# Two transformer blocks with hierarchical experts: the experts worked in pairs, their rows gathered four experts at a time, their weights loaded in 2 MB transfers

## The chip, the core and the metric

One NeuronCore of a Trainium2 chip runs the whole program in one launch. The metric is the device time of that launch in microseconds; lower is better. The kernel before was run three times.

## What is computed

The reference is two transformer blocks, one after the other, on 256 tokens of 1024 features, in float32. The first block has two layers (gated spatial mixing, then forgetting attention, each with attention to a memory and a convolutional feed-forward layer). The second has a gated delta rule and a retention mixer, an output projection, and then the layer that this change is about: a mixture of 64 experts in 8 groups, of which each token uses two.

```python
g_idx = jnp.argmax(hf @ w_router_group, axis=-1)            # one group per token
top_p, top_i = lax.top_k(e_prob, 2)                         # two experts inside it
expert_id = (g_idx[:, None] * 8 + top_i).reshape(-1)
order = jnp.argsort(expert_id); xs = ht[order // 2]
gate = lax.ragged_dot(xs, w_gate, group_sizes)              # [64, 1024, 256]
up   = lax.ragged_dot(xs, w_up, group_sizes)                # [64, 1024, 256]
y    = lax.ragged_dot(jax.nn.silu(gate) * up, w_down, group_sizes)   # [64, 256, 1024]
out  = jnp.zeros_like(ht).at[tok].add(y * weights[order][:, None])
return rms_norm(x + out, final_norm)
```

All 64 experts' weights are read: 3 matrices of 1 MB each, 192 MB in all.

## The kernel before, in words

The program is written tile by tile; a scheduler places the instructions of the dense part, while the experts' loop is issued in the order written (`tc.manual_schedule()`). The dense part (the first block and the second block's mixers) streams 1 MB weight units on the SP queue through a ring of two places (`load_unit`, L104), splits each into a high and a low part on ScalarE and VectorE (L118, L119), and multiplies on TensorE with three products per pair of operands (L246 to L248, L288 to L290, L862 to L864).

The experts (`experts`, from L1390) have places of their own for weights: 22 places of 8 KB per partition (1 MB each). 17 of them lie on the right side of SBUF in six pools (`XGROUPS`), opened in the order `XORDER` as the dense part's tiles there die; two are the dense ring's, two (`XA`) lie where dense tiles end, and the last (`XQ`) lies where the routing's tiles end. `more(n)` issues the loads in the order `seq`: gate and up of expert e, then down of expert e-1. Load i takes place i modulo 22, so it waits on SP until the last reader of load i-22 is done. All these loads are issued at L1446 on the SP queue, one after the other; the last expert's in halves at L1451.

`route` (L1602 on) finds each token's two experts and the token's rank in each, as a key 1024 e + rank (L1716). Then for each expert e, `expert(e)` runs these steps of the class `Experts`, 32 rows (`CAP`) each:

- `pick` (L1768 to L1791, VectorE): a one-hot column for each row, times the norm's factor, and another times the row's weight.
- `rows` (L1793, TensorE L1800): gathers the rows with 8 float32 products, four side by side in the array, each a quarter of the features; ScalarE copies them out (L1803). `rows_T` (L1805): two transposes (L1811) put features on partitions, VectorE applies the gain (L1814).
- `gate_up` (L1818, TensorE L1826): 32 float32 products, [128 x 32] by [128 x 128], four side by side; ScalarE copies them out (L1829).
- `turn` (L1841): a transpose (L1846) and two products that put the rows' weights on every partition (L1848). `act` (L1851): silu on ScalarE (L1856), two multiplications on VectorE (L1857, L1858), which write every row twice.
- `down` (L1862, TensorE L1870): four float32 products, [128 x 64] by [128 x 512], two side by side: 64 columns are 32 rows, each there twice. ScalarE and VectorE (L1874, L1875) make of the two copies a high and a low part.
- `sel` (L1878, GpSimd L1884, L1885): which token each row belongs to. `scatter` (L1888, TensorE L1894): four float32r products add the rows to the sums over the experts, which stay in four PSUM banks.

The order inside `expert(e)` is gate_up(e), rows(e+1), turn(e), act(e), down(e-1), loads, rows_T(e+1), scatter(e-2).

An expert with over 32 rows needs `overflow`, a conditional block between experts 40 and 41 (`EOVF`). It claims five places (`OVT`), so up to there `more` issues five loads fewer than there are places. A float32 product is two instructions in the trace (the 32 products of L1826 are 64), a transpose and a float32r product are one.

`finish` (L1509 on) takes the last norm from the PSUM sums and stores the output.

Of the kernel before, what the change touches and what calls it, by code (L numbers as in the profile page):

```python
# [12 lines left out]
F32 = mybir.dt.float32  # L13
# [23 lines left out]
EARLY = 2  # L37
# [6 lines left out]
XGROUPS = (2, 2, 4, 4, 2, 3)  # L44
XORDER = (2, 3, 1, 4, 0, 5)
XA = 2
XQ = 1
EOVF = 40
OVT = 5
# [4 lines left out]
class Builder:  # L54
# [3 lines left out]
    # ---------------------------------------------------------------- setup  # L58
    def setup(self):
        tc, nc, ctx = self.tc, self.nc, self.ctx  # L60
        self.ring = ctx.enter_context(tc.tile_pool(name="ring", bufs=RING))
# [13 lines left out]
    def dense_pools(self, ctx):  # L75
        tc = self.tc
        self.cp = ctx.enter_context(tc.tile_pool(name="cp", bufs=1))
        self.hps = [ctx.enter_context(tc.tile_pool(name="hpa", bufs=1, side="right"))]
        # the split weights, in two pools: the last units do with the first
# [42 lines left out]
    def mark(self, *engines):  # L122
        """the last instructions so far of engines, for behind()."""
# [4 lines left out]
    def behind(self, marks):  # L128
        """what is traced here is issued behind the marks on their engines."""
# [5 lines left out]
    def rsqrt(self, y, v):  # L135
        """y = v ** -0.5."""
# [20 lines left out]
    def squares(self, src, n, **tag):  # L157
        """the sum of the squares of src(t), [128, n], per token."""
# [13 lines left out]
    def row_bc(self, rs, pool, name):  # L172
        """rs [128 tok, tile] as a row [tok] on every partition."""
# [9 lines left out]
    def rstd(self, src, pool, name):  # L183
        """1 / rms of src(t) [128, 1024]: per token, and as a row on every partition."""
# [3 lines left out]
    def scaled(self, dst, ps, rb, mul=1.0):  # L188
        """dst = ps [128 f, 2, 256 tok] * mul * rb."""
# [11 lines left out]
    def to_feat(self, xn, outs, ks=(0, KC)):  # L201
        """xn(t, k) [128 tok, 128]; outs: (gain [128, 8], (hh, hl))."""
# [9 lines left out]
    def split_feat(self, pt, k0, g, h):  # L212
        """two feature chunks pt [128, 2, 256] under a gain, split."""
# [7 lines left out]
    def x_T(self, gain, h=None, half=None):  # L221
        """the residual under a gain, features on partitions, split; the norm's factor is left to its products."""
# [6 lines left out]
    def x_T_by_half(self, gain):  # L229
        """for the end of an output projection: the next layer's input, half by half."""  # L230
# [9 lines left out]
    def mm_feat(self, ps, w, h, c):  # L240
        """ps [128 f, 256 t] for column chunk c of a unit."""
# [15 lines left out]
    def tok_unit(self, ap, h):  # L257
        """[128 tok, tile, 256 f]; the unit's halves are halves of the contraction."""
# [20 lines left out]
    def out_chunks(self, w, chunks, first, last, halves=(0, 1)):  # L279
        """accumulate feature chunks [(hi, lo)] ([128, 256]) times their rows of a unit, bank by bank."""  # L280
# [11 lines left out]
    def out_last(self, w, chunks, first, nxt):  # L292
        """the last unit: each half of the features joins the residual when it is done."""
# [21 lines left out]
    # ------------------------------------------------------- memory attention  # L315
# [51 lines left out]
    def softmax_parts(self, lg, parts):  # L367
        """lg PSUM [128, n]; parts (start, end) are normalised each; returns SBUF [128, n]."""
# [18 lines left out]
    def attn(self, chunk, q, k, v, parts, done, extra=None, late=False):  # L387
        """two heads of a chunk, in steps: queries and keys of its pair of chunks, v [128, 2, 128]; parts the keys of
# [1637 lines left out]
```

## Time and profile before

| | |
|---|---|
| median of 3 runs | 1313.18 us (1312.6 to 1313.52) |
| profiled execution, span from its first to its last instruction | 1311.2 us |
| median less span (launch and end around the span) | 2.0 us |
| instructions | 29064 |
| TensorE busy | 1218.8 us (93%) |
| TensorE weight loads | 984.9 us (75%) |
| VectorE busy | 824.7 us (63%) |
| ScalarE busy | 579.4 us (44%) |
| GpSimd busy | 201.4 us (15%) |
| read from HBM | 327.21 MB |

Of the profiled execution the page gives the span alone. A busy share is a mean over stages with different limits; the experts are the last 480 us. A PE row of the timeline gives the start of a group of instructions and how long it was in the pipeline; as groups overlap, the difference of two starts is what a group costs.

### The profile page before, as it was taken

The page shows a single profiled execution, that of the slowest core. Times are in us where ns is not written, and L with a number is a line of the kernel's source. Part 1 is how long each engine was busy: PE and PEld are TensorE (multiplying, and loading weights), DVE is VectorE, ACT ScalarE, POOL GpSimd, SP SyncE. Part 2 cuts the span into 40 slices and gives each one's busy share as a digit, 9 for nine tenths or more (in the row PEclk, how much of TensorE's full clock was granted, in tenths as well). Part 3 has the DMA queues.
Part 4 walks back from the last instruction along what each step waited for, and adds up shares of the span by engine and source line. Part 5 has one row for each costly group of instructions (what it writes and reads, how often), then busy time and mean ns, then how long its engine had stood idle before and what let it go on. Part 6 is the DMA issues. An engine that isn't in the chain of part 4 may idle for free.

```text
span 1311.2 us, 29064 instructions
## 1 busy us (share of the span) xinstructions
PE 1218.8 (93%) x12119; PEld 984.9 (75%) x12119; DVE 824.7 (63%) x1845; ACT 579.4 (44%) x1053; POOL 201.4 (15%) x190
## 2 busy tenths in 40 slices
PE   8999999999999999999999999888888888788895
PEld 7889999998888999999889988555454555455553
DVE  6867877777766777777778666544444444334443
ACT  7756555556655655555573444322222222121222
POOL 0100000000200000000322000323333332223230
PEclk9999999999999999999899999999999999899998
DMA  8534455553324655555422377899999999999970
GB/s 289 184 117 170 175 187 190 193 193 131 131 93 139 254 192 189 193 181 195 143 97 97 130 294 297 339 419 418 419 417 419 417 418 418 362 406 418 417 295 33
DMA packets 49753, 330.16 MB, mean 252 GB/s; under 512 B 6704, under 2 KB 8240, under 8 KB 10832
## 3 DMA queue, kind: packets, MB, share of 16 engines
q1 hardware_dynamic: 48512, 326.55, 64.4%
q8 instruction: 97, 1.59, 0.5%
q0 software_dynamic: 528, 1.21, 0.3%
q10 hardware_dynamic: 576, 0.49, 0.1%
q14 instruction: 40, 0.33, 0.1%
HBM read 327.21 MB, written 1.05 MB: 250 GB/s over the span
## 4 chain that ended last, share of the span: by engine, by line
PE 78%; DVE 11%; ACT 5%; DMA 3%; issue 2%; POOL 1%; SPq 0%; DVEq 0%; ACTq 0%; POOLq 0%
PE g L1826 9%; PE bank L1870 9%; PE oacc L288 5%; PE oacc L290 5%; PE oacc L289 5%; PE g L1800 4%; PE g L248 3%; PE g L246 3%; PE g L247 3%; DVE y L1875 3%; PE bank L247 3%; PE bank L246 3%; PE bank L248 3%; ACT hs L1874 3%; PE g L862 2%
## 5 line engine op out<-in xcount | busy, mean ns | idle before, releaser
L119 DVE TENSOR_TENSOR wl<-wraw,wh 128x1024 fp32r<-128x1024 f32 x230 | 282.3, 1230 | 91.3 <-ACT wh L118 90.0
L118 ACT CAST wh<-wraw 128x1024 fp32r<-128x1024 f32 x230 | 240.2, 1051 | 217.1 <-PE g L247 73.6
L1826 PE MATMUL g<-wraw,xw 128*32 128x128 f32 x4096 | 126.8, 276 | 55.2 <-DVE xw L1814 49.8
L1826 PEld LDWEIGHTS g<-wraw,xw 128*32 128x32 f32 x4096 | 109.4, 111 | 82.1 <-DVE xw L1814 74.8
L246 PE MATMUL g<-hh,wh 128*128 128x256 f32 x448 | 126.9, 284 | 0.3 <-ACT hh L216 0.3
L248 PE MATMUL g<-hh,wl 128*128 128x256 f32 x448 | 126.5, 283 | 0.6 <-DVE wl L119 0.6
L247 PE MATMUL g<-hl,wh 128*128 128x256 f32 x448 | 126.3, 282 | 0.0
L1870 PE MATMUL bank<-wraw,hm 128*64 128x512 f32 x512 | 124.0, 605 | 0.9 <-DVE y L1875 0.5
L1875 DVE SCALAR_TENSOR_TENSOR y<-bank,part,hs 128x512 fp32r<-128x512 f32 x64 | 48.1, 751 | 117.0 <-ACT hs L1874 117.0
L1884 POOL TENSOR_SCALAR s<-krow,tgt 128x512 bf16<-128x512 f32 x64 | 106.3, 1660 | 24.1 <-ACT krow L1740 12.0
L1829 ACT COPY gu<-g 128x128 f32<-128x128 f32 x64 | 17.0, 265 | 205.0 <-PE g L1826 205.0
L246 PE MATMUL bank<-hh,wh 128*128 128x256 f32 x352 | 99.2, 282 | 0.0
L247 PE MATMUL bank<-hl,wh 128*128 128x256 f32 x352 | 99.0, 281 | 0.0
L248 PE MATMUL bank<-hh,wl 128*128 128x256 f32 x352 | 99.0, 281 | 0.0
L1857 DVE TENSOR_TENSOR h<-h,bank 128x64 f32<-128x64 f32 x64 | 14.2, 222 | 132.9 <-ACT h L1856 132.9
L1874 ACT ACTIVATE hs<-bank,part 128x512 fp32r<-128x512 f32 x64 | 44.0, 687 | 108.3 <-PE bank L1870 108.3
L1885 POOL TENSOR_TENSOR sl<-s 128x256 fp32r<-128x256 bf16 x64 | 42.7, 667 | 297.9 <-PE mo L1894 297.5
L246 PEld LDWEIGHTS g<-hh,wh 128*128 128x128 f32 x448 | 85.0, 190 | 1.8 <-ACT hh L216 0.5
L248 PEld LDWEIGHTS g<-hh,wl 128*128 128x128 f32 x448 | 85.1, 190 | 0.9 <-DVE wl L119 0.8
L247 PEld LDWEIGHTS g<-hl,wh 128*128 128x128 f32 x448 | 85.0, 190 | 1.1 <-issue 0.2
L862 PE MATMUL g<-hh,wh 128*128 128x256 f32 x272 | 79.8, 294 | 1.9 <-ACT qs L983 1.4
L864 PE MATMUL g<-hh,wl 128*128 128x256 f32 x272 | 77.6, 286 | 1.2 <-DVE wl L119 1.2
(560 smaller groups left out, 2787.4 us busy)
## 6 DMA issues: line engine op xcount, KB each, us to landing
wraw<-in_w_gate_dram SPq DMA_DIRECT2D x63, 1024.0 KB, 16.2
wraw<-in_w_up_dram SPq DMA_DIRECT2D x63, 1024.0 KB, 14.8
wraw<-in_w_down_dram SPq DMA_DIRECT2D x63, 1024.0 KB, 16.9
wraw<-in_a_ffn_in_dram SPq DMA_DIRECT2D x22, 1024.0 KB, 4.8
wraw<-in_b_ffn_in_dram SPq DMA_DIRECT2D x22, 1024.0 KB, 4.8
wraw<-in_w_in_dram SPq DMA_DIRECT2D x16, 1024.0 KB, 5.0
wraw<-in_a_ffn_out_dram SPq DMA_DIRECT2D x11, 1024.0 KB, 4.7
wraw<-in_b_ffn_out_dram SPq DMA_DIRECT2D x11, 1024.0 KB, 4.8
```

Source lines behind the costliest of these rows:

```text
L118: self.nc.scalar.copy(wh, r)
L119: self.nc.vector.tensor_tensor(wl, r, wh.bitcast(F32), op=OP.subtract)
L246: nc.tensor.matmul(ps, wh[:, k], hh[:, k], start=k == 0, stop=False)
L247: nc.tensor.matmul(ps, wh[:, k], hl[:, k], start=False, stop=False)
L248: nc.tensor.matmul(ps, wl[:, k], hh[:, k], start=False, stop=k == KC - 1)
L862: nc.tensor.matmul(ps, wh[:, k], hh[:, k], start=k == 0, stop=False)
L864: nc.tensor.matmul(ps, wl[:, k], hh[:, k], start=False, stop=k == KC - 1)
L1826: nc.tensor.matmul(pg[n * C:(n + 1) * C], xw[:, k % 2, k // 2], ws[n // 2][:, k, n % 2 * P:][:, :P], start=k == 0, stop=k == KC - 1)
L1870: nc.tensor.matmul(py[h * 64:(h + 1) * 64], hm[:, j].rearrange("p a c -> p (a c)"), d3[:, j, h * 512:(h + 1) * 512], start=j == 0, stop=j ...
L1874: nc.scalar.activation(hs, py, AF.Copy, scale=m.part[:, 0:1])
L1875: nc.vector.scalar_tensor_tensor(y, py, m.part[:, 1:2], hs.bitcast(F32), op0=OP.mult, op1=OP.subtract)
L1884: nc.gpsimd.tensor_scalar(s1, m.krow, tgt, None, op0=OP.is_equal)
```

## The change

Weights: gate and up of an expert become one array of 16 KB per partition (`w_gu_2`), and the two down matrices of a pair of experts another (`w_down_2`). One transfer moves 2 MB, in rows of 16 KB. There are 11 places of 16 KB per partition: nine in five pools on the right, one where dense tiles end, one where the routing's tiles end. The ring of the dense part is no longer one of them; it moves into the dense part's pools. The scratch space for descriptors of GpSimd's DMAs shrinks to 1 KB (`SCRATCH`); two of the ten mask planes go, two selector operands being read as broadcast columns of another plane.

```diff
-XGROUPS = (2, 2, 4, 4, 2, 3)
-XORDER = (2, 3, 1, 4, 0, 5)
-XA = 2
-XQ = 1
-EOVF = 40
-OVT = 5
+XGROUPS = (1, 1, 3, 2, 2)
+XORDER = (2, 1, 3, 4, 0)
+XLATE = 1
+PAIRS = 32
+POVF = 20
+OVT = 4
+SCRATCH = 1024
...
-            u64, b64, sel0, sel1 = (cm[:, i] for i in range(4))
+            u64, b64 = cm[:, 0], cm[:, 1]
+            sel0, sel1 = (b64[:, i:i + 1].to_broadcast([P, P]) for i in (0, 64))
...
+            seq = [(0, 0), (1, 0)]
+            for e in range(2, NE, 2):
+                seq += [(e, 0), (e + 1, 0), (e - 2, 1)]
+            seq[-2:] = [(NE - 4, 1), (NE - 1, 0), (NE - 2, 1)]
```

The last two of the 96 loads go in halves of 1 MB. The loop works on pairs:

```diff
+            def pair(p):
+                a, b = 2 * p, 2 * p + 1
+                if p:
+                    X.sel(p - 1)
+                X.gate_up(a)
+                if p < PAIRS - 1:
+                    X.gate_up(b)
+                    if p % 2:
+                        X.gather(p // 2 + 1)
+                    if p > 1:
+                        X.scatter(p - 2)
+                    X.turn(a)
+                    X.turn(b)
+                    X.act(a)
+                    X.act(b)
+                    if p:
+                        X.down(p - 1)
+                else:
...
+                    X.gate_up(b)
+                    X.scatter(p - 1)
+                    X.turn(b)
+                    X.act(b)
+                    X.down(p)
+                more(3 * p + 2 + len(slots) - (OVT if p <= POVF else 0))
...
             with tc.manual_schedule():
-                for e in range(EOVF):
-                    expert(e)
-                    X.pick(e + 2)
-                expert(EOVF)
+                for p in range(POVF + 1):
+                    pair(p)
+                    if p % 2 == 0:
+                        X.pick(p // 2 + 1)
             self.overflow(m, X, [slot() for _ in range(OVT)])
```

The overflow block stands after pair 20 (experts 40 and 41) and claims four places. The steps:

```diff
+    def gather(self, q, n=4):
+        nc, b, s = self.nc, self.b, self.s.pop(q)
+        self.xw[q] = xw = self.kept("xw", NT * n * CAP, [KC, n * CAP], bufs=1)
+        g = b.gain("ffn_norm_2")
+        for i in range(2):
+            ks = range(i * KC // 2, (i + 1) * KC // 2)
+            px = b.bank([P, KC // 2, n * CAP])
+            for k in ks:
+                for t in range(NT):
+                    nc.tensor.matmul(px[:, k - ks[0]], b.x[:, t, k * P:(k + 1) * P], s[:, t], start=t == 0,
+                                     stop=t == NT - 1)
+            nc.vector.tensor_tensor(xw[:, ks[0]:ks[0] + KC // 2], px,
+                                    g[:, ks[0]:ks[0] + KC // 2][:, :, None].to_broadcast([P, KC // 2, n * CAP]),
+                                    op=OP.mult)
...
     def turn(self, e):
-        pt = self.b.bank([P, 5, CAP])
-        nc.tensor.transpose(pt[:, 0:4].rearrange("p a c -> p (a c)"), self.gu, self.b.ident)
-        for t in range(NT):
-            nc.tensor.matmul(pt[:, 4], self.m.onesf, s[:, 3, t], start=t == 0, stop=t == NT - 1)
+        self.pt[e] = pt = self.b.bank([P, 4, CAP])
+        self.nc.tensor.transpose(pt.rearrange("p a c -> p (a c)"), self.gu.pop(e), self.b.ident)
...
+    def down(self, p):
+        hms = [self.hm.pop(2 * p + i) for i in range(2)]
...
+        py = self.b.bank([P, 512], "g")
+        for j in range(2):
+            for n in range(4):
+                h, e = n // 2, n % 2
+                nc.tensor.matmul(py[n * C:(n + 1) * C], hms[e][:, j], d[:, e, j, h * 512:(h + 1) * 512],
+                                 start=j == 0, stop=j == 1)
+        w = self.weight(p)
+        hi, lo = (self.kept(t, o, [512], F32R, 1) for t, o in (("yh", 768), ("yl", 1280)))
+        nc.scalar.activation(hi, py, AF.Copy, scale=w)
+        nc.vector.scalar_tensor_tensor(lo, py, w, hi.bitcast(F32), op0=OP.mult, op1=OP.subtract)
...
+        nc.vector.scalar_tensor_tensor(junk, m.krow, tgt, m.wrow, op0=OP.is_equal, op1=OP.mult,
+                                       accum_out=self.weight(p))
```

So `gather` brings four experts' rows with features on partitions at once (16 float32 products of 128 columns), without copy and transposes; `pick` makes one-hot columns for four experts in six VectorE operations; `sel` also sums each row's weight on VectorE (the diff's last operation); `gate_up` is unchanged but for its operands; `down` does two experts at once, four products of 32 columns side by side; `scatter` adds the high and the low part in eight products per pair. `route` makes a second row array (`wrow`, the weights) beside `krow`, with four more float32 products, and gathers the first four experts before the first pair.

## Rows read from the trace of the kernel before

**Rows 1.** The page's second part: granted TensorE clock, DMA share (tenths) and GB/s in 40 slices of 32.8 us.

```profile
PEclk9999999999999999999899999999999999899998
DMA  8534455553324655555422377899999999999970
GB/s 289 184 117 170 175 187 190 193 193 131 131 93 139 254 192 189 193 181 195 143 97 97 130 294 297 339 419 418 419 417 419 417 418 418 362 406 418 417 295 33
```

**Rows 2.** Busy time by stretch: start and end in us, length, busy us of each engine with its instructions, then granted clock, DMA share, GB/s. The first is the end of the mixers, in which the experts' places open; the next four are the experts; then two earlier stretches.

```profile
747.00:834.00 87.00, 81.91 (x624) 71.39 (x622) 58.80 (x199) 38.77 (x65) 4.40 (x11) 1.00 0.76 292
840.00:1120.00 280.00, 246.21 (x3857) 144.91 (x3855) 121.76 (x389) 60.11 (x155) 87.02 (x75) 1.00 1.01 417
1120.00:1160.00 40.00, 31.10 (x422) 18.08 (x426) 14.31 (x46) 7.10 (x18) 11.77 (x11) 0.91 0.92 362
1160.00:1260.00 100.00, 88.46 (x1382) 51.91 (x1374) 43.05 (x138) 21.67 (x56) 31.73 (x28) 1.00 1.01 418
1260.00:1270.00 10.00, 8.43 (x171) 5.73 (x175) 5.34 (x18) 1.56 (x5) 4.64 (x4) 1.00 0.90 362
640.00:660.00 20.00, 16.28 (x112) 15.21 (x111) 13.82 (x47) 10.80 (x18) 5.68 (x2) 0.83 0.31 110
10.00:20.00 10.00, 9.53 (x67) 9.16 (x67) 9.64 (x34) 9.53 (x17) 0.65 (x1) 1.00 0.93 336
```

**Rows 3.** Timeline of TensorE over one expert in the loop: start, time in the pipeline, instructions; in brackets the idle time before and what ended it.

```profile
1029.92 1.95 PE L1826 MATMUL g<-wraw,xw 128*32 128x128 f32 x64 [0.87 <-DVE xw L1814]
1031.69 1.04 PE L1800 MATMUL g<-x,s 128*32 128x256 f32 x16
1032.67 0.33 PE L1846 MATMUL bank<-ident,gu 128*128 128x128 f32 x1
1032.83 0.53 PE L1848 MATMUL bank<-s,onesf 128*128 128x32 f32 x4
1033.29 1.94 PE L1870 MATMUL bank<-wraw,hm 128*64 128x512 f32 x8
1035.16 0.44 PE L1811 MATMUL bank<-ident,xr 128*128 128x128 f32 x2
1035.53 0.73 PE L1894 MATMUL mo<-y,sl 64*128 64x512 f32 x4
1037.14 0.43 PE L1826 MATMUL g<-wraw,xw 128*32 128x128 f32 x8 [0.88 <-DVE xw L1814]
```

**Rows 4.** The largest sum of waits of TensorE between 840 and 1270 us: who for whom, us in total, times, longest.

```profile
PE g L1826 <- DVE xw L1814: 49.8, 57, 0.9
```

**Rows 5.** The SP queue's issues of the experts' loads: the gate matrices by line (count, ns of one, first and last start); then from the timeline, with the start of each, ten issues in a row (the first and the last) and those on both sides of the overflow block.

```profile
L1446 SPq DMA_DIRECT2D wraw<-in_w_gate_dram x63: 327/328/426, 423.9 to 1235.9; - x63
...
1073.31 0.33 SPq L1446 DMA_DIRECT2D wraw<-in_w_gate_dram  x1
...
1095.76 0.33 SPq L1446 DMA_DIRECT2D wraw<-in_w_gate_dram  x1
...
1114.74 0.33 SPq L1446 DMA_DIRECT2D wraw<-in_w_up_dram  x1
1131.88 0.33 SPq L1446 DMA_DIRECT2D wraw<-in_w_down_dram  x1
```

**Rows 6.** TensorE at the same place, the last step before the block and the first after it, and the chain that ended last there (start, us, what).

```profile
1122.13 0.73 PE L1894 MATMUL mo<-y,sl 64*128 64x512 f32 x4
1128.21 3.64 PE L1826 MATMUL g<-wraw,xw 128*32 128x128 f32 x64 [5.35 <-DMA wraw<-in_w_up_dram]
1131.60 0.69 PE L1800 MATMUL g<-x,s 128*32 128x256 f32 x4
...
1114.74 13.46 DMA wraw<-in_w_up_dram
```

**Rows 7.** TensorE at the end of the routing and the start of expert 0, and the SP queue's last load before.

```profile
827.27 1.07 PE L1800 MATMUL g<-x,s 128*32 128x256 f32 x16 [0.37 <-DVE late L1727]
829.10 1.06 PE L1738 MATMUL bank<-ident,key 128*128 128x128 f32 x8
830.08 1.96 PE L1826 MATMUL g<-wraw,xw 128*32 128x128 f32 x64
...
826.37 0.33 SPq L1446 DMA_DIRECT2D wraw<-in_w_up_dram  x1
```

**Rows 8.** The end: the last expert's last matrix and its scatter, which the last norm follows up to the span's end.

```profile
1296.02 1.94 PE L1870 MATMUL bank<-wraw,hm 128*64 128x512 f32 x8 [0.28 <-issue]
1299.61 0.73 PE L1894 MATMUL mo<-y,sl 64*128 64x512 f32 x4 [1.65 <-DVE y L1875]
```

**Rows 9.** The page's third part (queue, kind: packets, MB, share of 16 engines) and three lines of its sixth (issues: count, KB each, median us from issue to landing).

```profile
q1 hardware_dynamic: 48512, 326.55, 64.4%
q8 instruction: 97, 1.59, 0.5%
wraw<-in_w_gate_dram SPq DMA_DIRECT2D x63, 1024.0 KB, 16.2
out_dram<-x SPq DMA_DIRECT2D x3, 256.0 KB, 3.0
g<-in_final_norm_dram POOLq DMA_DIRECT2D x4, 128.0 KB, 4.3
```

**Rows 10.** The longest wait of TensorE between 640 and 660 us.

```profile
PE sm L1123 <- DVE rsc L1105: 3.2, 1, 3.2
```

More of the change, by code (lines that the diff above doesn't have):

```diff
@@ L36 @@
 NLATE = 6
-EARLY = 2
 T2 = 3
@@ L1431, in experts @@
+            early = len(slots)
             taken = itertools.count()
-            def place(pool, tag):
-                return pool.tile([P, 2048], F32, name="wraw", tag=tag)
             def slot():
-                return place(*slots[next(taken) % len(slots)])
+                return slots[next(taken) % len(slots)].tile([P, 4096], F32, name="wraw", tag="wraw")
             def more(n):
-                while len(m.loads) < min(n, 3 * NE):
+                while len(m.loads) < min(n, len(seq)):
@@ L1455, in experts @@
-            xa = ctx.enter_context(tc.tile_pool(name="moea", bufs=XA, reuse_waits="tile"))
-            slots[-1:-1] = [(xa, "wraw")] * XA
-            more(len(slots))
+                    t = m.loads[e, k] = slot()
+                    if i < len(seq) - 2:
+                        src = A["w_down_2"][e // 2] if k else A["w_gu_2"][e]
+                        with self.behind(self.mark(nc.sync) if 0 < i < early else []):
+                            nc.sync.dma_start(t, src)
+                        continue
@@ L1504, in experts @@
-                X.scatter(NE - 1, True)
+                for p in range(POVF + 1, PAIRS):
+                    pair(p)
+                    if p % 2 == 0 and p < PAIRS - 2:
+                        X.pick(p // 2 + 1)
+                X.scatter(PAIRS - 1, True)
                 self.finish(m, X, m.fin)
@@ L1722, in route @@
         sums(SV[2])
-        X.pick_rows(0)
-        X.rows(0)
+        X.pick(0)
+        X.gather(0)
         sums(SV[3])
@@ L1862, in down @@
-    def down(self, e):
-        nc, m = self.nc, self.m
-        hm = self.hm.pop(e)
-        d3 = self.load(e, 2).rearrange("p (k f) -> p k f", k=2)
-        py = self.b.bank([P, 512])
-        for j in range(2):
-            for h in range(2):
-                nc.tensor.matmul(py[h * 64:(h + 1) * 64], hm[:, j].rearrange("p a c -> p (a c)"),
-                                 d3[:, j, h * 512:(h + 1) * 512], start=j == 0, stop=j == 1)
-        hs = self.wk.tile([P, 512], F32R, name="hs", tag="hs", bufs=1)
-        y = self.kept("y", 640, [512], F32R)
-        nc.scalar.activation(hs, py, AF.Copy, scale=m.part[:, 0:1])
-        nc.vector.scalar_tensor_tensor(y, py, m.part[:, 1:2], hs.bitcast(F32), op0=OP.mult, op1=OP.subtract)
-        self.yy[e] = y
@@ L1888, in scatter @@
-    def scatter(self, e, last=False):
+        junk = self.wk.tile([P, 2, S], BF, name="junk", tag="junk", bufs=1)
+        nc.vector.scalar_tensor_tensor(junk, m.krow, tgt, m.wrow, op0=OP.is_equal, op1=OP.mult,
+                                       accum_out=self.weight(p))
+    def scatter(self, p, last=False):
         nc = self.nc
-        sl, y = self.sl.pop(e), self.yy.pop(e)
+        sl, y = self.sl.pop(p), self.yy.pop(p)
         for t in range(NT):
-            for h in range(2):
-                hs = slice(h * 64, h * 64 + 64)
-                nc.tensor.matmul(self.m.oacc[t][h], sl[hs, t * P:(t + 1) * P], y[hs], start=False, stop=last)
+            for i in range(2):
+                for h in range(2):
+                    hs = slice(h * 64, h * 64 + 64)
+                    nc.tensor.matmul(self.m.oacc[t][h], sl[hs, t * P:(t + 1) * P], y[i][hs], start=False,
+                                     stop=last and i == 1)
```

262 lines of the change are left out of this document (102 added, 160 removed).

## The prediction

> **What bounds the kernel now.** I read the slices first, then the stretches, then one expert in the timeline, then the SP queue, then the end. The slices show two regimes: up to about 750 us the DMA engines are half idle, from about 850 they move 417 to 419 GB/s in nearly every slice, the one dip being at 1115 to 1180 [rows 1]. So the experts' stage (830 to 1300 us, over a third of the time) seems bound by its loads. The timeline says otherwise. One expert takes TensorE 1037.14 - 1029.92 = 7.22 us and it never waits for a load, only 0.87 us per expert for VectorE's gain, 49.8 us in all [rows 3, 4]. The loads are a little slower: ten issues in a row that waited only for earlier loads stand (1095.76 - 1073.31) / 9 = 2.494 us apart, so three matrices take 7.48 us [rows 5]. TensorE gains 0.26 us per expert on a stock of loaded places, and the stock lasts but for one stop, at the overflow block: the last load issued before it (1114.74) lands at 1128.21, and that is when TensorE goes on, after 5.35 us idle; no load is issued from 1114.74 to 1131.88 [rows 5, 6]. After it loads stay ahead. They end near 1269 (the stretch 1260 to 1270 still moves 362 GB/s [rows 2]), while TensorE works until 1299.61 + 0.73 = 1300.3 and the span ends at 1311.2 [rows 8]. **Two limits of nearly equal length lie side by side; today TensorE ends last, 42 us behind the loads.** A change to TensorE's work can win no more than that lag, less what must follow the last byte.
>
> **TensorE's work, per pair of experts.** A group's cost is the difference of starts [rows 3], unless said otherwise.
> - Gate and up: as before, 2 x 1.77 = 3.54.
> - Gather: 16 products, 32 instructions, for four experts. The nearest row is the float32 products of the key, 8 instructions in 0.98 us [rows 7], so 3.92, per pair 1.96. What goes are L1800 (0.98 per expert, the same array work), the two transposes (0.37) and the wait for the gain (0.87).
> - Turn: the transposes stay, 2 x 0.16; the weights' products (0.46 per expert) go.
> - Down: 16 instructions instead of 8 per expert. Two side by side cost 1.87 for 8. The gate products already run four side by side at 1.77/64 us per 128 columns, which is 1.77 for these 16; without any gain from four it would be 3.74. I take 1.87.
> - Scatter: eight per pair, today four per expert, so unchanged: 2 x 0.73 = 1.46 at most.
>
> Sum 9.15 us per pair, today 14.43. Upper bound with a down that gains nothing and two waits like today's: 12.8. The other engines have room whatever the new steps cost: today VectorE is busy 121.76 of 280 us, GpSimd 87.02, ScalarE 60.11 [rows 2], and all three lose steps per expert (GpSimd does its two once per pair); VectorE gains one, the weights' sum.
>
> **The loads become the bound.** 192 units of 1024 KB (1.049 MB, below "units") remain, now moved two at a time. I follow them to their end.
> - Start. The places hold 22 units before and after. The first loads go out at 424 us [rows 5], the others as the mixers end (DMA share 0.76 from 747 to 834 [rows 2]), and before the last place's load is issued at 826.37 [rows 7]. I take the same openings; all 22 units are then in by the time an expert ends, so an earlier place brings nothing. The first place comes free later: the first gather starts at 827.3 as now, takes 3.9 us for four experts, the key's and the weights' 16 instructions take 2.0, gate and up of expert 0 start at 833.2 instead of 830.08, and its place is free at 835.0 [rows 7].
> - From there 170 units are left: 170 x 2.494 = 424.0 us. The fixed part of a transfer counts once: 256 KB land in 3.0 us [rows 9], of which 0.6 is bytes, so 2.4.
> - Rows of 16 KB instead of 8: no row shows a weight load with them. A stretch with rows of 4 KB and less among the others moved 336 GB/s at share 0.93, 361 at a full share, against 417/1.01 = 413 [rows 2]: shorter rows cost 13%, small ones included. A gain of up to 3% (13 us) is the one end. The other is the instruction loads on queue 8, 97 packets of 16.4 KB at 0.005 x 16 x 1311.2 / 97 = 1.08 us [rows 9], 15 GB/s per engine where queue 1 has 24; these run beside queue 1's packets, which they must wait for, so the end is excluded as a likely price and kept as a rival. I take 0, nearest to the spacing row.
> - Overflow. Today the stop costs the DMA engines (418 - 362) x 40 / 418 = 5.4 us [rows 2]. After the change more(n) allows seven loads (14 units, 14 x 2.494 = 35 us) beyond pair 20, so TensorE will stand about that long until all have landed, as it did for one unit today. It has the slack, but nothing is under way when it starts again: load 69 needs the place of expert 42, free 3.7 us after the restart as today (1131.88 - 1128.21). Places come back at TensorE's pace, two units at a time; I add 2 us: 7.4. Ends: 0 and 20 (a whole pair at the low clock plus a landing).
>
> Last landing: 835.0 + 2.4 + 424.0 + 7.4 = 1268.8, about where the loads end today.
>
> **After the last byte.** Today 15.2 us pass from the last down's first product to the end [rows 8]. Now the last half of a down, four abreast, is 0.93 instead of 1.87; eight scatters instead of four add about 0.4. TensorE will have waited before it. Here the trace shows what waits do: after a wait of 3.2 us between 640 and 660 the mean clock of that stretch is 0.83 [rows 2, 10], after the 5.35 us the 64 gate products take 3.39 us instead of 1.77 [rows 3, 6], the low level (1.2 of 2.4 GHz). I add 1.9 for the end at the low level: 16.5. **Span 1268.8 + 16.5 = 1285.3, that is 25.9 less than the profiled 1311.2.** The median of the runs stands 2.0 us above that span, so 1287.
>
> At nothing I cost: the two broadcast columns (four small products), the mask planes, the ring's new address; the two units that the dense ring holds cover them. GpSimd's smaller descriptor space could hold up its seven loads; the nearest row is 4.3 us to landing for a norm's gain [rows 9]: 0 to +5, taken 0, as TensorE has the mixers' products beside it.
>
> The Trainium skill (DMA: Bandwidth & Descriptors, Bandwidth) gives 425 GB/s for a 16 MB transfer and 341 for one of 1 MB, issued from GpSimd; by its 425 the 170 units (178.3 MB) would take an estimated 419.5 us, 4.5 less than taken, and the end would be 1283. The trace has 418 with 1 MB transfers already, as they queue behind each other [rows 2].
>
> **Rivals.**
> 1. *The places starve the loads* (18%). A place of two units opens only when all that lay there is dead, and after the overflow TensorE hands back places too slowly. For it: the share of 0.76 before 834 shows that openings limit the start [rows 2]. Against: 22 units by 835 need only 55 us of DMA time. Price: 20 instead of 7.4 at the block, or up to 7 us at the start; about 1300.
> 2. *TensorE at the low clock* (6%), the one on the other side. Now every load is waited for, 5 us apart, with gaps near 3 us. If the array stays at 1.2 GHz, a pair costs 9.15 x 3.39/1.77 = 17.5 us and TensorE is the bound: 833.2 + 32 x 17.5 + 11.6 (scatter to end [rows 8]) = 1404.8, 1407 with the 2.0. It decides from a mean of (1311.2 - 833.2 - 11.6) / 32 = 14.6 us per pair on, about 65% of the time at the low level. Against: a TensorE that falls behind has no gaps, and in the busy stretches after both stops the clock is back at 1.00 [rows 2]. The Trainium skill (TensorE: Matmul & The Clock Gate, HAM oscillation) describes this case: groups of matmuls shorter than the wait for the next load each start throttled. By that rule alone all pairs would cost the low price; the two stops agree with it, the stock of places speaks against its lasting.
> 3. *The long rows are slower* (4%). Then the transfer doesn't do what it is named for. At queue 8's price it would be far slower, 178.3 MB at 16 x 15.2 GB/s being 733 us; it takes a rate 6% lower (424 us become 450) to eat all that is won. I give half of this to no change.
>
> **How the numbers follow.** My forecast has 72%: 1287, by itself 1275 to 1297. Its low side: no loss at the block (-7.4), no low clock at the end (-1.9), a little from the longer rows. Rival 1 carries the range upward to 1304, a full gain from the rows (13 us) downward to 1273; outside lie rivals 2 and 3 and the tails. This kernel's runs can tell 0.2% (2.6 us) from no change. Faster: 72 + 18 + 2 of rival 3 = 92%; same 2%; slower 6%.
>
> **What would show it.** Right: the stretches from 840 on at 418 GB/s or more but for one dip near the overflow block; TensorE busy well under the 88% of today; its waits now for loads, not for VectorE; in one pair groups of about 3.5, 1.9, 1.5 us; gather beginning near 827; the last load landing 16 to 17 us before the end; some slices with a clock below 1. Wrong: a load rate that differs by over 3%; waits of SP for places in mid-stage; TensorE without waits, or slices at the low clock one after the other; an end over 20 us after the last landing; a dense part that no longer ends near 820.

## The result, and the profile after

| | before | after |
|---|---|---|
| median of the runs | 1312.89 us (4 runs) | 1282.74 us (4 runs, 1282.48 to 1283.66) |
| ratio | | 0.9778, 95% interval 0.9758 to 0.9798 |
| span of the profiled execution | 1311.2 us | 1280.9 us |
| first gather, seen in the trace | 827.27 us | 828.23 us |
| from the first gather to the span's end | 483.9 us | 452.7 us |

The change is 30 us faster; forecast were 26, and 1287 us. The last row matters below: the dense part ahead of the experts ends at another time in each profiled execution (the first gather starts anywhere from 823.2 to 830.5 us in the runs of this study), so kernels that differ only in the experts' stage are compared from the first gather on.

The page's second part, 40 slices of 32.0 us (answers to [rows 1]), and the fourth part, the chain of work that ended last:

```profile
PE   7999999999999999999989999989876767577665
...
PEclk8999999999999999999989999999997998888987
DMA  8524555554323665555523146889999999999994
GB/s 279 201 99 167 190 178 192 194 176 158 132 100 132 239 258 196 176 188 187 186 93 132 67 170 239 334 356 423 425 425 425 426 425 426 422 424 426 426 424 186
...
DMA 11%; PE 2%; DVE 0%; ACT 0%; issue 0%; DVEq 0%; ACTq 0%; SPq 0%
```

TensorE's busy digits fall to 5 to 7 from some 930 us on; from 840 to 1120 us it is busy 74% of the time (first row below), where [rows 2] have 88%. The chain that ended last is DMA with 11% of the span and TensorE with 2%. It goes back no further than the overflow block (the last 13% of the span), while in the kernel before it covers the whole span, TensorE having 78% and DMA 3%. The dip of 362 GB/s is gone. Stretches (columns as in [rows 2]):

```profile
840.00:1120.00 280.00, 208.37 (x3582) 156.28 (x3578) 69.19 (x204) 32.17 (x104) 46.61 (x42) 0.91 1.01 425
1120.00:1160.00 40.00, 29.25 (x494) 20.93 (x486) 9.08 (x27) 5.37 (x16) 6.96 (x7) 0.87 1.01 425
1160.00:1250.00 90.00, 62.28 (x1020) 46.69 (x1020) 19.56 (x57) 9.35 (x30) 13.39 (x12) 0.89 1.01 425
1250.00:1260.00 10.00, 8.29 (x100) 5.91 (x101) 1.60 (x5) 1.76 (x4) 0.67 (x1) 0.83 0.85 347
1260.00:1270.00 10.00, 8.17 (x104) 4.20 (x102) 1.46 (x5) 2.27 (x6) 0.00 (x0) 1.00 0.24 95
```

425 GB/s from 840 to 1250 without a break, where [rows 2] have 417 and 362. TensorE's longest sums of waits from 840 to 1270 (who for whom, us, times, longest), where [rows 4] had VectorE's gain:

```profile
PE g L1817 <- DMA wraw<-in_w_gu_dram: 81.7, 34, 3.3
PE g L1855 <- DMA wraw<-in_w_down_dram: 11.1, 10, 1.7
PE g L1817 <- DVEq L1543: 9.7, 1, 9.7
PE g L1817 <- issue: 5.8, 5, 1.8
```

93 us of waits for loads: TensorE has slack. (DVEq L1543 is VectorE's sequencer at the branch of the overflow block; "issue" is idle time for which the profile shows no reason.) One pair in TensorE's timeline (as [rows 3]; L1817 gate and up, L1801 gather, L1885 scatter, L1835 turn, L1855 down):

```profile
986.66 3.64 PE L1817 MATMUL g<-wraw,xw 128*32 128x128 f32 x64 [3.35 <-DMA wraw<-in_w_gu_dram]
990.23 4.32 PE L1801 MATMUL bank<-s,x 128*128 128x128 f32 x32
994.47 0.50 PE L1885 MATMUL mo<-yh,sl 64*128 64x512 f32 x2
...
995.60 0.44 PE L1835 MATMUL bank<-ident,gu 128*128 128x128 f32 x2
995.96 1.92 PE L1855 MATMUL g<-wraw,hm 128*32 128x512 f32 x16
997.71 1.93 PE L1817 MATMUL g<-wraw,xw 128*32 128x128 f32 x64
1001.20 1.95 PE L1817 MATMUL g<-wraw,xw 128*32 128x128 f32 x64 [1.57 <-DMA wraw<-in_w_gu_dram]
```

Down for two experts costs 997.71 - 995.96 = 1.75: four abreast gain what they gain in the gate. Behind the wait of 3.35 us the gate takes 3.57 us instead of 1.8, the low level; before the pair is over the clock is back. The end (as [rows 8]): the last half of the last down, then the last scatter.

```profile
1266.01 1.07 PE L1855 MATMUL g<-wraw,hm 128*32 128x512 f32 x8 [0.36 <-DMA wraw<-in_w_down_dram]
...
1269.29 0.40 PE L1885 MATMUL mo<-yl,sl 64*128 64x512 f32 x2
```

The last load has landed when TensorE goes on at 1266.0, and 14.9 us later the span ends. **The loads now set the end.**

### The profile page after: what moved, and what is told of

It is laid out like the page before. It is cut to its first block, busy times and chain, and to the rows that moved or that the text cites. A ratio compares the mean times of both kernels' runs of the same rounds, so it can differ in the third digit from the quotient of the medians.

```text
span 1280.9 us, 26452 instructions
## 1 busy us (share of the span) xinstructions
PE 1134.8 (89%) x11231; PEld 985.9 (77%) x11231; DVE 727.4 (57%) x1501; ACT 531.7 (42%) x958; POOL 122.0 (10%) x126
## 5 line engine op out<-in xcount | busy, mean ns | idle before, releaser
L1817 PE MATMUL g<-wraw,xw 128*32 128x128 f32 x4096 | 152.3, 310 | 97.4 <-DMA wraw<-in_w_gu_dram 81.7
L1817 PEld LDWEIGHTS g<-wraw,xw 128*32 128x32 f32 x4096 | 135.8, 125 | 128.7 <-issue 117.9
L248 PE MATMUL g<-hl,wh 128*128 128x256 f32 x448 | 126.3, 282 | 0.0
L1803 DVE TENSOR_TENSOR xw<-bank,gains 128x512 f32<-128x512 f32 x32 | 22.1, 692 | 133.4 <-PE bank L1801 133.4
L864 PE MATMUL g<-hl,wh 128*128 128x256 f32 x272 | 77.6, 286 | 0.0
L1843 DVE TENSOR_TENSOR hm<-h,bank 128x64 f32<-128x64 f32 x64 | 11.6, 218 | 115.2 <-ACT h L1842 115.2
L597 DVE SCALAR_TENSOR_TENSOR hc<-hr,cw,hc 128x254 f32<-128x254 f32 (+1 forms) x176 | 73.5, 478 | 0.8 <-ACT hc L594 0.7
L1855 PE MATMUL g<-wraw,hm 128*32 128x512 f32 x512 | 62.6, 598 | 11.1 <-DMA wraw<-in_w_down_dram 11.1
L1860 DVE SCALAR_TENSOR_TENSOR yl<-g,wr_m,yh 128x512 fp32r<-128x512 f32 x32 | 24.0, 751 | 81.6 <-ACT yh L1859 81.6
## 6 DMA issues: line engine op xcount, KB each, us to landing
wraw<-in_w_gu_dram SPq DMA_DIRECT2D x63, 2048.0 KB, 39.2
wraw<-in_w_down_dram SPq DMA_DIRECT2D x31, 2048.0 KB, 39.2
```

Source lines behind the costliest of these rows:

```text
L248: nc.tensor.matmul(ps, wh[:, k], hl[:, k], start=False, stop=False)
L597: nc.vector.scalar_tensor_tensor(hv[:, c, sh:], hr[:, c, :S - sh], cw[:, 2 - sh, f:f + 1], hv[:, c, sh:], op0=OP.mult, op1=OP.add)
L864: nc.tensor.matmul(ps, wh[:, k], hl[:, k], start=False, stop=False)
L1817: nc.tensor.matmul(pg[n * C:(n + 1) * C], xw[:, k], ws[:, n // 2, k, n % 2 * P:][:, :P], start=k == 0, stop=k == KC - 1)
L1855: nc.tensor.matmul(py[n * C:(n + 1) * C], hms[e][:, j], d[:, e, j, h * 512:(h + 1) * 512], start=j == 0, stop=j == 1)
L1860: nc.vector.scalar_tensor_tensor(lo, py, w, hi.bitcast(F32), op0=OP.mult, op1=OP.subtract)
```

## The experiments

**1. TensorE alone.** In both kernels the later loads are left out, and with them the right weights: experts multiply with what lies in a few places.

```diff
# kernel after
+                    if i >= early:
+                        m.loads[e, k] = m.loads[seq[4 + i % 6]]
+                        continue
# kernel before
+                    if i >= n0:                          # n0 = 21
+                        m.loads[e, k] = m.loads[seq[5 + i % 16]]
+                        if e == NE - 1 and not k:
+                            m.fin = slot()[:, :D]
+                        continue
```

> The kernel after with only the first ten 2 MB loads; every later expert multiplies with weights that already lie in one of six of those places. What is left is TensorE's own pace. My theory (the pair costs TensorE about 9.15 us, and the loads set the end of the kernel after): 32 pairs from 833 us on at 9.15 us, 12 us behind them and some 6 us at the overflow block, a span of 1140 to 1150 us against 1280.9. Rival A (TensorE falls to the low clock and stays there, 17.5 us per pair): 1405. Rival B (TensorE still sets the end, the gain came from elsewhere): no shorter than 1275.

> The kernel before with only the first 21 loads; every later expert multiplies with weights that already lie in one of 16 of those places. My theory (TensorE ends last in the kernel before, its loads run ahead): 7.22 us per expert as before, a time of 1306 to 1313, that is at most 0.6% under the kernel before. If the loads set the end of the kernel before: about 42 us less or more than that is not possible from the lag, but every wait for a load would go; a loads-bound kernel would fall by far over 2%. A second question hangs on it: with no load in flight at the overflow block, a stop of TensorE that stays near 5.4 us belongs to the branch itself, one that goes belonged to a load's landing (the prediction took it so).

Measured: 1135.85 us (one run, span 1134.2) for after, 1310.65 for before (ratio 0.9991, 0.9978 to 1.0005). Without its loads the kernel before takes its usual time: it was bound by TensorE. The kernel after falls by 147 us: it is bound by loads. Its span lies 6 us under the expected range, as TensorE's pairs are shorter than taken. TensorE's timeline of after without loads, two gathers two pairs apart being the period's ends:

```profile
1040.04 3.84 PE L1804 MATMUL bank<-s,x 128*128 128x128 f32 x32
...
1057.70 2.50 PE L1804 MATMUL bank<-s,x 128*128 128x128 f32 x20
```

17.66 / 2 = 8.83 us per pair; predicted were 9.15.

**2. More work on TensorE, first dose.** Each product of gate and up twice; then those of down twice as well.

```diff
# a_gate2, in gate_up
+        for _ in range(2):
             for k in range(KC):
                 for n in range(4):
...
# a_gate2_down2, in down as well
-        for j in range(2):
+        for j in (0, 1, 0, 1):
             for n in range(4):
```

> The kernel after with every product of gate and up done twice (3.54 us more of TensorE per pair, 113 us in all; same result). My theory (loads at 4.92 us per 2 MB, 14.76 per pair, set the pace; TensorE with 9.15 + 3.54 = 12.7 per pair stays under it): only the first expert's doubled products show, the first place coming free 1.8 us later, and perhaps as much after the last byte: 1284 to 1288. Rival (TensorE's work or its waits set the pace): 1282.7 + 113 = 1396, or a good part of it.

> The kernel after with the products of gate and up and those of down done twice (3.54 + 1.75 us more per pair: 14.4 us, the 14.43 of the kernel before). My theory: TensorE then ends last again. From 833 us 32 pairs at 14.4, some 6 us at the block, 12 to 15 us behind them: a span of 1312 to 1316, so the time of the kernel before comes back (1313 to 1318) although the loads move as in the kernel after. Rival (the gain came from the 2 MB loads): at most 1290.

Measured: 1354.39 (ratio 1.0306) and 1377.85 (1.0516). Both expectations missed, by 66 and 60 us beyond their upper ends. TensorE's products have no wait for a load left, but pauses with no releaser, here at 999.67, 1009.29 and 1015.42 (doubled gate and up; the sum is from 840 to 1330):

```profile
999.67 1.07 PE L1818 MATMUL g<-wraw,xw 128*32 128x128 f32 x13 [2.60 <-issue]
...
1004.90 2.58 PE L1818 MATMUL g<-wraw,xw 128*32 128x128 f32 x87
1009.29 3.70 PE L1818 MATMUL g<-wraw,xw 128*32 128x128 f32 x128 [1.81 <-issue]
1015.42 1.45 PE L1818 MATMUL g<-wraw,xw 128*32 128x128 f32 x41 [2.43 <-issue]
```

```profile
PE g L1818 <- issue: 69.1, 38, 3.2
```

In the records of the single packets a 16 KB packet of the instruction queue (queue 8) starts at 997.21, 1006.89 and 1013.16, and TensorE goes on 2.3 to 2.5 us behind each. The same holds of all 25 pauses of its products over 1.5 us from 840 to 1330 (the block's stop aside): each ends 2.2 to 2.6 us behind the start of such a packet. So a new theory: TensorE had run out of instructions, which come over the DMA engines that the weights keep full.

**3. The same dose in few instructions, and the first dose without loads.** Down done three times, then four times; and the doubled gate and up of experiment 2 with the edit of experiment 1.

```diff
# a_down3 (a_down4: * 4), in down
-        for j in range(2):
+        for j in (0, 1) * 3:
             for n in range(4):
```

> The kernel after with the products of down done three times: 3.5 us more of TensorE per pair, the same dose as the doubled gate and up, but in 32 instructions of 512 columns per pair in place of 128 of 128 columns. Theory 1 (the loads set the pace, and the doubled gate and up fell short of it because TensorE waited for its own instructions, which come in packets of 16 KB over the DMA engines that the loads keep full): TensorE's own time would be 1135.9 + 32 x 3.5 = 1248, under 1282.7, so the time stays at 1282 to 1288 and TensorE's idle time without a releaser stays near the 6 us of the kernel after. Theory 2 (any 3.5 us more of TensorE per pair costs, as TensorE's waits add to its work): about 1354, as with the doubled gate and up.

> Down done four times: 5.25 us more per pair, 14.1 us in all, about the 14.43 of the kernel before. Theory 1: TensorE's own time is 1135.9 + 32 x 5.25 = 1304, now over 1282.7, so TensorE ends last: 1304 to 1312, most of what the change had won is gone with the loads as they are. Theory 2: 1385 or more. If the gain came from the 2 MB loads: at most 1290.

> Gate and up done twice, and the loads after the first ten left out (later experts use weights that already lie in six of the places). Theory 1 (TensorE's pauses without a releaser in the doubled gate and up are its instruction loads queueing with the weight loads): they vanish with the weight loads, 1135.9 + 113 = 1249. Theory 3 (the pauses belong to the long run of 256 products itself, whatever the DMA engines do): they stay, some 70 us more, about 1320.

Measured: 1287.40 (0.9822, 0.9799 to 0.9845), 1309.84 (0.9988, 0.9971 to 1.0005) and 1252.93 (one run). All three as theory 1 has it. TensorE's longest wait between 840 and 1270 with down three times, the first stretch with down four times (columns as in [rows 2]), and TensorE in the doubled gate and up without loads, where the 256 product instructions of a pair run without a break:

```profile
PE g L1817 <- DMA wraw<-in_w_gu_dram: 17.2, 8, 3.3
```

```profile
840.00:1120.00 280.00, 278.01 (x4336) 161.65 (x4324) 63.83 (x189) 30.68 (x100) 44.20 (x40) 1.00 1.01 425
```

```profile
980.61 7.17 PE L1821 MATMUL g<-wraw,xw 128*32 128x128 f32 x256
```

So 3.5 us more per pair, 112 us in all, cost 5 us, and from the first gather on 7.8 (1285.1 - 824.61 = 460.5): the last load is issued 408.3 us behind the first gather, 407.8 in the kernel after, and what is added lies behind it, where the last two downs are done three times (7 us). TensorE's waits shrink instead. At 5.25 us more, 14.1 per pair, TensorE ends last again and the time of the kernel before is back, though the loads move 425 GB/s from 840 to 1120. The gain is TensorE's, up to the point where the loads take over. The first dose cost more than its work because of its instructions: the pauses go when the weight loads go. From the first gather on the doubled gate and up takes 524.7 us beside the loads and 421.6 without. Of these 103 us the pauses are 69; an estimated 20 more are products at the low clock behind them (the mean granted clock is 0.95 from 840 to 1330, against 0.99 from 840 to 1240 without loads). The rest is open.

**4. The overflow block left out** (its places are still claimed; no expert here has over 32 rows).

```diff
-            self.overflow(m, X, [slot() for _ in range(OVT)])
+            [slot() for _ in range(OVT)]
```

> The kernel after without the conditional overflow block (its four places are still claimed, so that the loads' places are the same; the experts with more than 32 rows would lose them, but none has). My theory now: the stop of TensorE at the block costs nothing in the kernel after, as eight loads are under way and the loads go on: 1281.5 to 1283. The prediction's step (the block costs the loads 7.4 us): 1275.

Measured: 1281.48 (0.9765, 0.9749 to 0.9782); from the first gather to the end 1282.5 - 829.70 = 452.8, after 452.7. The block costs nothing. Why, in the trace of after (SP's issues around the block, TensorE and VectorE there; columns as before):

```profile
1086.00 0.33 SPq L1442 DMA_DIRECT2D wraw<-in_w_down_dram  x1
1090.90 17.12 SPq L1442 DMA_DIRECT2D wraw<-in_w_gu_dram  x2
```

```profile
1096.10 1.92 PE L1855 MATMUL g<-wraw,hm 128*32 128x512 f32 x16 [1.67 <-DMA wraw<-in_w_down_dram]
1107.74 5.13 PE L1817 MATMUL g<-wraw,xw 128*32 128x128 f32 x128 [9.72 <-DVEq L1543]
```

```profile
1107.57 0.75 DVE L1875 SCALAR_TENSOR_TENSOR junk<-krow,tgt,wrow 128x512 bf16<-128x512 f32 x1 [6.23 <-DVEq L1543]
```

TensorE stands 9.7 us, not 35, and not for a load: behind the stop it runs two experts' gates without a break, though their loads land some 4.9 us apart. By the trace it waits for VectorE, which idles 6.2 us at the branch of L1543; TensorE, VectorE and SP all go on within 0.2 us of each other, so which of them held the others is inferred, not shown. Without loads TensorE still stands 6.2 us there (first line below). SP issues nothing for 16.8 us (its second issue is at 1107.70), but a load takes 39.2 us from issue to landing, eight under way, and the DMA engines do not notice: their share from 1090 to 1108 is 1.01. The branch in three other traces (TensorE behind it in after without loads; then VectorE behind it: before, before without loads, after without loads):

```profile
PE g L1820 <- DVEq L1546: 6.2, 1, 6.2
```

```profile
1128.97 0.17 DVE L1779 TENSOR_SCALAR kk<-key 128x4 f32<-128x4 f32 x1 [5.29 <-DVEq L1540]
```

```profile
1123.73 0.17 DVE L1785 TENSOR_SCALAR kk<-key 128x4 f32<-128x4 f32 x1 [2.54 <-DVEq L1546]
```

```profile
1017.23 0.29 DVE L1792 TENSOR_SCALAR s<-s,rs_m 128x128 f32<-128x128 f32 x1 [3.28 <-DVEq L1546]
```

5.3 and 6.2 us beside the weight loads, 2.5 and 3.3 without. The other traces agree: 6.1 to 6.3 us where loads fill the DMA engines at the block (down three times, rows of 8 KB, shorter look-ahead), 3.2 to 3.9 where few or none are under way there (down four times and the three runs with the doubled gate). TensorE stops at the block in the kernel before without loads, too: the two experts on both sides take 20.07 us (from 1114.03 to 1134.10) instead of 2 x 7.22, in the kernel before 21.49 (1116.52 to 1138.01). So 5.6 of the 7.0 us that it loses there are the branch's, without any load; that the load of [rows 6] landed as it went on is at most a small part of it.

**5. Rows of 8 KB in the kernel after.**

```diff
-                            nc.sync.dma_start(t, src)
+                            for c in (slice(0, 2048), slice(2048, 4096)):
+                                nc.sync.dma_start(t[:, c], src[:, c])
```

> The kernel after with each 2 MB place filled by two transfers in rows of 8 KB instead of one in rows of 16 KB; all else as in the kernel after. Theory 1 (a row of 16 KB takes 612 to 614 ns on a DMA engine, two of 8 KB 2 x 312, and that is all there is to the longer rows): 2.494 instead of 2.460 us per MB, 170 of them, 5.8 us more: 1287 to 1290, 418 GB/s in the experts' stretches. Rival (the gain of the change came from the 2 MB transfers): most of the 30 us gone, 1305 or more. If the rows do nothing at all: 1282 to 1283.

Measured: 1285.44 (0.9806, 0.9785 to 0.9826); from the first gather on 1288.0 - 829.00 = 459.0, 6.3 more than after. The median is a little under the expected range, and its interval overlaps that of the change, so the reading rests on the profiled executions; those of after, of experiment 4 and of experiment 6 agree within 0.1 us. The stretch that answers to the first of the fence on stretches:

```profile
840.00:1120.00 280.00, 215.58 (x3536) 155.38 (x3536) 67.38 (x201) 32.31 (x105) 45.26 (x41) 0.90 1.01 418
```

418 GB/s again. The long rows are worth 1.7% of rate and 6 us, a fifth of the gain.

**6. A shorter look-ahead.**

```diff
-                more(3 * p + 2 + len(slots) - (OVT if p <= POVF else 0))
+                more(3 * p + 2 + len(slots) - 6)
```

> The kernel after with loads issued at most as far ahead as six places less than there are, from the first pair to the last (in the kernel after: four less up to the overflow block, none behind it), so that two to five loads are under way at the end instead of eight. Theory U1 (the DMA engines have rates of their own, packets of 612 to 621 ns, and the slowest sets the last landing however deep the queue is): the same time within 2 us, the issues a little further apart (4.95 to 4.97 us) and the engines done closer together at the end. Theory U2 (the deep queue lets the engines drift apart and costs the last landing some 5 us): 1277 to 1279. Rival 1 of the prediction (too few places starve the loads): 1290 or more, with dips of the DMA share in mid-stage.

Measured: 1279.33 (0.9763, 0.9742 to 0.9783), but in the profiled execution 1277.0 - 824.20 = 452.8 from the first gather on, as after: its gain lies ahead of the experts. And the edit did not do what I meant: TensorE goes on with the last load, issued at 1232.07, at 1262.20, 30.1 us later, 29.9 in the kernel after. `more` only fixes the order of SP's issues; when they go out, the places decide. It says nothing on U1 and U2.

**7. The start.** First the rearrangement with a gather of 64 columns, then a smaller one.

```diff
# a_start
-        X.gather(0)
+        X.gather(0, cols=slice(0, 2 * CAP))
...
                     X.gate_up(b)
+                    if not p:
+                        self.rows_of_keys(m)
+                        X.gather(0, cols=slice(2 * CAP, 4 * CAP))
# a_early
                 X.gate_up(a)
+                if not p:
+                    self.rows_of_keys(m)
```

`rows_of_keys` holds the loop that made `krow` and `wrow` at the end of `route`.

> The kernel after with its start rearranged: the first gather brings only the first pair's 64 columns, expert 0 and 1 follow at once, and the key's and the weights' rows and the other 64 columns come behind them. Theory (the stream of loads stands still from 832 us until the first place comes free at 837.3, and everything behind it hangs on that): the first place is free at 833 to 834, the last landing and the end come 3 to 4 us earlier, 1278 to 1280. Rival (the loads' end is set by the DMA engines' total work and the gap at the start is filled by loads that are still landing): 1282 to 1283.

> The kernel after with one step moved: the products that make the key's and the weights' rows (16 instructions, 2.0 us) stand behind the first expert's gate and up, not among them; the first gather stays whole, with 128 columns. Theory (the stream of loads stands still until the first place is free, and this rearrangement of the start, unlike the one with 64 columns, leaves TensorE no narrow products and no new wait ahead of it, so its granted clock stays at 1.00): the first place comes free 2.0 to 2.4 us earlier (6.7 to 7.1 us behind the start of the first gather, not 9.1), and the span's end stands 450.3 to 450.7 us behind the start of the first gather, not 452.7; the time falls by 2 us, about 1280.5, which the medians alone can hardly show. If the start does not matter: 452.7 us again. If the clock falls as it did with 64 columns: 453 to 455.

Measured: 1281.46 (0.9772, 0.9751 to 0.9794) and 1279.72 (0.9756, 0.9735 to 0.9777); from the first gather on 454.6 and 451.2. TensorE there, of after, of the first and of the second:

```profile
828.23 2.02 PE L1801 MATMUL bank<-s,x 128*128 128x128 f32 x16 [0.77 <-DVE s L1789]
...
833.02 1.06 PE L1817 MATMUL g<-wraw,xw 128*32 128x128 f32 x26
834.01 1.16 PE L1746 MATMUL bank<-ident,key 128*128 128x128 f32 x8
835.00 1.06 PE L1746 MATMUL bank<-ident,w 128*128 128x128 f32 x8
835.99 3.04 PE L1817 MATMUL g<-wraw,xw 128*32 128x128 f32 x102
```

```profile
828.25 1.97 PE L1812 MATMUL bank<-s,x 128*128 128x64 f32 x16 [0.77 <-DVE s L1794]
830.74 3.50 PE L1812 MATMUL bank<-s,x 128*128 128x64 f32 x16 [0.52 <-DVE xw L1814]
834.16 5.44 PE L1828 MATMUL g<-wraw,xw 128*32 128x128 f32 x128
```

```profile
825.86 2.02 PE L1805 MATMUL bank<-s,x 128*128 128x128 f32 x16 [0.77 <-DVE s L1793]
...
830.65 1.95 PE L1821 MATMUL g<-wraw,xw 128*32 128x128 f32 x64
832.53 1.16 PE L1518 MATMUL bank<-ident,key 128*128 128x128 f32 x8
```

The first bought nothing: 64 columns took as long as 128 for the first eight products (1.97 against 2.02), then the granted clock stood at 0.62 from 830 to 834 and 0.53 to 838, and the first place came free at 837.87. The second kept the clock at 1.00: the first place is free 832.66 - 825.86 = 6.8 us behind the first gather, 9.1 in the kernel after, and of these 2.3 us 1.4 reach the end (expected 2.0 to 2.4; the last scatter ran at the low level). Its ratio is the lowest here (that of experiment 6 is 0.9763, at a median of 1279.33), but its interval overlaps that of the change, and the 1.4 us rest on one profiled execution of each.

## Why the prediction was right, and where not

- **What bounds before.** Right, and shown: without loads nothing changes (experiment 1).
- **TensorE per pair.** 9.15 taken, 8.83 measured. Down at 1.75 (1.87), scatter 995.60 - 994.47 = 1.13 (1.46 at most), turn 0.36 (0.32), gate and up as before.
- **The loads become the bound.** Right, shown by experiments 1 and 3. The working from 827.3 gave the last landing 441.5 us behind the first gather; it came 437.7 behind it. The pieces of that, one by one:
  - Start. First place free 7.7 us behind the first gather, measured 9.1: the gather takes 4.8 (833.02 - 828.23) instead of 3.9, 0.78 of it a wait for the gain between its halves, and the first gate with the two rows' products 4.3 instead of 3.8 (up to the issue at 837.33). +1.4. That all was in by then was right: the DMA share from 834 to 838 is 0.02. The issue for the first free place:

```profile
837.33 2.08 SPq L1442 DMA_DIRECT2D wraw<-in_w_gu_dram  x2
```

  - **Rows of 16 KB, taken at 0.** Twelve loads on, SP's issues stand (1205.36 - 1146.30) / 12 = 4.92 us apart (rows below), 2.461 us per unit against 2.494: 170 x 0.033 = -5.6, inside the end of -13 that the text kept.

```profile
1146.30 0.33 SPq L1442 DMA_DIRECT2D wraw<-in_w_down_dram  x1
...
1205.36 0.33 SPq L1442 DMA_DIRECT2D wraw<-in_w_down_dram  x1
```

  - **Overflow block, taken at 7.4: the step that failed.** It said that TensorE stands some 35 us until all issued loads have landed and that nothing is under way then. The runs show a stop of 9.7 us that comes with the branch, loads that never stop, and the same time without the block, 452.8 us against 452.7 (experiment 4). The error was to take the releaser that the chain of waits infers in [rows 6] for the cause, and to read the DMA engines' dip of the kernel before, where 13 us of loads were under way, into one with 39. -7.4.
  - The end of the stream, not in the sum. The DMA engines do not finish together: their mean share falls to 0.85 in the last stretch but one and to 0.24 in the last (fence above). 9.1 + 85 x 4.92 + 2.4 = 429.7 against 437.7, so about +8.0. That the engines' own rates do it (single packets take 612 to 621 ns) is argued, not shown; rows of 8 KB, with 20 us between the last issue and its use instead of 30, have such an end too (a share of 0.59 from 1265 to 1270). The last two loads, in halves, go in rows of 4 KB: their packets take some 161 ns, four of them 644 where one of 16 KB takes 614, which makes an estimated 0.5 us of it.
- **After the last byte.** 16.5 taken, 14.9 measured: TensorE had the last norm's gain and the last expert's gate to do while the last load landed, so that the 1.9 for the low clock was not due (granted clock 1.00 from 1260 to 1270 in the trace above).
- **Sum.** +1.4 - 5.6 - 7.4 + 8.0 - 1.6 = -5.2: 452.8 from the first gather on, where 458.0 was forecast and 452.7 measured. Of the +8.0 only the share of the last two stretches is seen directly; the rest closes the sum. Errors of 15 us one way and 9 the other made a forecast that was 4 us off: that it came so near is luck in part, not the working's merit.
- **Rival 2, the low clock.** What it names happens: granted clocks of 0.91, 0.87 and 0.89, the gate behind a wait at half speed (986.66). The Trainium skill (TensorE: Matmul & The Clock Gate, HAM oscillation) describes that much. Its price did not come, as the prediction argued: a mean of 0.89 is the low level for 22% of the time, where the rival needed 65%, and TensorE that is late has no waits.
- **Rival 1, starved places.** From 830 on only at the start (834 to 837.3). **Rival 3, slower rows:** the opposite, 16 KB of weights in 614 ns. It was set aside rightly, but the reason given, that queue 8's packets are slow because they wait for queue 1's, does not hold: from 840 to 1120 they take a median of 1.07 us in the kernel after and 0.99 without loads.

## What to carry to other kernels

Before costing a change, find by how much the second limit lies behind the first: here 42 us of lag set the most that TensorE's relief could give, and the loads took over after 30. A releaser that a trace infers is a candidate, not a cause; ask what else ended at the same moment. And compare small edits from a mark just ahead of them: here the medians vary by more in what lies ahead than the edits are worth.

## What the runs showed of the hardware

- **Instructions compete with loads.** With the DMA engines at 392 GB/s, a run of 512 instructions (the 256 of a pair's doubled gates and their weight loads, 7 us of work) made TensorE pause 38 times, up to 3.2 us, 69.1 us in all, each pause over 1.5 us ending 2.2 to 2.6 us behind the start of an instruction packet. Without loads there is no such pause; 112 us of work in long products came with 2.0 us of them. The packets themselves take no longer beside the loads (a median of 0.97 us, 1.04 without), so what holds the instructions up lies ahead of their transfer; what it is stays open. The Trainium skill (Runtime: NRT & Kernel Launch, Instruction fetch mechanics) says that an engine's sequencer fetches blocks of 16 KiB by a DMA queue of its own and that this is mostly hidden. The kernel after agrees (5.8 us before its gates); the doubled gate beside the weight loads does not.
- **A branch costs more beside loads.** VectorE idles 2.5 to 3.9 us at it with few or no loads under way and 5.3 to 6.3 behind full queues, though the branch skips the block. The same section of the Trainium skill says that a taken branch out of the fetched window forces a fetch. The stops fit that, but no run here shows that the fetch is what they wait for.
- **Row length still counts at 8 KB.** 418 against 425 GB/s with deep queues, packets of 313 and 614 ns. The Trainium skill (DMA: Bandwidth & Descriptors, Bandwidth) has 425 for a 16 MB transfer; the kernel after shows that rate with 2 MB transfers that queue behind each other.
- **64 columns were no cheaper than 128** in float32 products whose weights are loaded anew each time (1.97 and 2.02 us for 16 instructions).
